# A wider gate product with token-major gates, and three orders moved, in an fp32 hybrid encoder layer

## The chip, the cores and the metric

The kernel runs on one core of a Trainium2 chip. The metric is the device time of one execution in microseconds. A core has a matrix engine (TensorE, PE in the profile; its weight loads are PEld), a vector engine (VectorE, DVE), a scalar engine (ScalarE, ACT), GpSimd (POOL) and SyncE (SP), which here issues nearly all DMAs. Each engine runs its own instructions in order and waits on the others by semaphores. Matrix products land in PSUM, everything else lies in SBUF; what does not fit goes through scratch tensors in DRAM.

## The reference

One encoder layer over 2048 tokens of width 1024, in float32. The input projection's columns go to two groups: group A (width 512) is a gated linear attention that runs in both directions, group B (width 512) a multi-head latent attention with four heads. Each group's output is multiplied by a SiLU gate, both are concatenated, and one output projection and a residual LayerNorm follow:

```python
h = x @ w_in
o_a = gla_branch(g_q, g_k, g_v, g_gate, ...)          # scans both ways, rms_norm, * silu(g_gate)
q  = rms_norm(c_q) @ w_uq;  kv = rms_norm(c_kv) @ w_ukv
p  = softmax(q_nope @ k_nope.T + rope(q_r) @ rope(k_r).T)
o_b = (p @ v) * silu(m_gate)
x  = layer_norm(ALPHA * x + concat(o_a, o_b) @ w_out)
```

The change touches m_gate, the gate of group B: its product with x, its SiLU, and its way to the output stage.

## The kernel before, in words

Every product is done in three matmuls, since each operand is split into a rounded high part and the rest: high·high, low·high and high·low (the helper `mm3`, L419 to L421; `hi` makes a high part on ACT, L365, `lo` the rest on DVE or POOL, L371). Tokens are cut into 16 chunks of 128.

The span has four parts. The first sweep (0 to about 348 us) goes over the chunks backwards and makes group A's inputs and states. The second sweep, `sweep_c` (about 348 to 580 us), takes two chunks at a time in eight steps. The attention (580 to about 1108 us) goes over blocks of 128 queries and pairs of key tiles. The output stage (about 1070 to 1263 us) takes the chunks one by one.

A step of the second sweep works on: `pz`, the gate product, in eight pieces; `ipm`, the product for c_q, c_kv and k_r; `Ob`, the output of group A, whose norm and gate make `og` and its transpose `oT`; `tm`, `cqT_h`, `cqT_l`, the transposed c_q; `pqr` and `pq`, the queries (`qah` and `qal` are the halves of pq). PSUM tiles pz, pq and Ob share a pool `gp` with two slots. The gate goes through ACT three times (`c_gm1` to `c_gm3`: Exp, Ln with bias 1, Exp, which is the sigmoid) and DVE once (`c_gm4`: times pz); `c_sgm` stores it to the scratch `gm_s`. In SBUF, gm and qal share one slot with the tag "gm"; og has two slots of its own.

The order of the second sweep is written as numbers: `PLACE_C` gives each operation a place, the step's number plus an offset (a pair holds the offsets of the step's two chunks, j = 0 and 1); `PLACE_C_FIRST` and `PLACE_C_LAST` replace some of them in the first and the last step. `sweep_c` sorts all operations by place and issues them in that order, and every engine keeps it.

In the output stage, `load` brings a chunk's two halves (`of`, group A from `oa_s` and group B from `ob_s`) and gate factors (`gr`, from `gm_s` and `r_s`, the reciprocal softmax sums) back from DRAM; `load_res` brings x (`xr`). `split` makes high and low parts (`oh`, `ol`) and multiplies by the gate on POOL. `product` runs 48 matmuls of 512 columns for each chunk, into `po` (odd chunks, both halves in one two-bank tile) or into `pmb` and `px` (even chunks, one bank each); `residual` adds x (`rr`), `finish` does the LayerNorm (`ln`) and stores. The last two query blocks' ends are threaded in: `sx` and `rc` (the sums and reciprocals of blocks 14 and 15), `rt` (the transposed reciprocals, made by `turn`), stored by `rows` to `r_s`. From chunk 4 on, `fixed` keeps the written order on ACT, POOL and SP; PE and DVE are placed by the scheduler, which follows an estimate of when things are ready. In the lists of rows below, a name ends in its chunk's, step's or block's number.

Of the kernel before, what the change touches and what calls it, by code (L numbers as in the profile page):

```python
# [135 lines left out]
STEP_C = ("gm1", "gm2", "gm3", "gm4", "sgm", "pq", "qah", "qal", "sqa")  # L136
# [3 lines left out]
    "ss", "rgl", "rgd", "og", "oT", "soT")  # L140
# [57 lines left out]
    gm1=0.823,  # L198
    gm2=0.832,
    gm3=0.837,  # L200
    gm4=0.845,
# [72 lines left out]
    gm1=0.643,  # L274
    gm2=0.815,
    gm3=0.82,
    gm4=0.83,
# [31 lines left out]
    ss=(0.166, 0.454),  # L309
# [4 lines left out]
    krf=(0.139, 0.6),  # L314
# [4 lines left out]
    xl=(-0.244, 0.3),  # L319
# [14 lines left out]
    gm1=1.309,  # L334
    gm2=1.608,
    gm3=1.859,
    gm4=1.953,
# [16 lines left out]
class K:  # L354
# [151 lines left out]
    def run(self):  # L506
        tc, nc, ins = self.tc, self.nc, self.ins
        with ExitStack() as top:
# [9 lines left out]
            self.gm_s = [dp.tile([P, H, QB], F32, name=f"gm_s{b}") for b in range(NQB)]  # L518
# [632 lines left out]
    def sweep_c(self):  # L1151


        with ExitStack() as ctx:
# [9 lines left out]
            def put(n, st, fn, *a, j=None):  # L1164
                last = st == len(steps) - 1
                p = PLACE_C[n]
                p = (last and PLACE_C_LAST.get(n)) or (not st and PLACE_C_FIRST.get(n)) or p
                todo.append((st + (p if j is None else p[j]), len(todo), fn, a))
# [88 lines left out]
    def c_pz(self, s, n):  # L1257
        last = s["st"] == NCH // 2 - 1
        if n == 0:
            s["pz"] = self.gp.tile([P, H, 256], F32, tag="gp", name=f"pz{s['st']}")  # L1260
        order = [(h, k) for h in range(H) for k in range(NK)]
        if last:
            order = [(h, k) for p in range(2) for k in range(NK) for h in (p, p + 2)]
        x2 = lambda t, k: t[:, k].rearrange("p a t -> p (a t)")
        part = [(h, k, p) for h, k in order[4 * n:4 * n + 4] for p in range(3)]
        if n == 0 and s["st"]:

            part.sort(key=lambda e: e[2] == 1)
        stop = {h: (k, p) for h, k, p in part if k == NK - 1}
        for h, k, p in part:  # L1270
            w, x = ((0, self.xch), (0, self.xcl), (1, self.xch))[p]
            self.nc.tensor.matmul(s["pz"][:, h], self.Wz[k][w][:, h * P:(h + 1) * P], x2(x, k),  # L1272
                                  start=(k == 0 and p == 0), stop=stop.get(h) == (k, p))

    def c_gm1(self, s):
        s["gm"] = self.w1.tile([P, H, 256], F32, tag="gm", name=f"gm{s['st']}")
        self.nc.scalar.activation(s["gm"], s["pz"], AF.Exp, scale=-1.0)

    def c_gm2(self, s):
        self.nc.scalar.activation(s["gm"], s["gm"], AF.Ln, bias=1.0)  # L1280

    def c_gm3(self, s):
        self.nc.scalar.activation(s["gm"], s["gm"], AF.Exp, scale=-1.0)

    def c_gm4(self, s):
        self.nc.vector.tensor_tensor(s["gm"], s["pz"], s["gm"], ALU.mult)
# [4 lines left out]
    def c_sgm(self, s):  # L1291
        b, qs = self.of_step(s)
        self.nc.sync.dma_start(self.gm_s[b][:, :, qs], s["gm"])
# [13 lines left out]
    def c_qal(self, s):  # L1307
        s["ql"] = self.w1.tile([P, H, 256], F32R, tag="gm", name=f"qal{s['st']}")
        self.lo(s["ql"], s["pq"], s["qh"])

    def c_sqa(self, s):
        b, qs = self.of_step(s)
        for t, dst in zip((s["qh"], s["ql"]), self.qa_s[b]):
            self.nc.sync.dma_start(dst[:, :, qs], t.bitcast(F32))
# [266 lines left out]
    def attention(self):  # L1581
# [4 lines left out]
        with ExitStack() as ctx:  # L1586
# [284 lines left out]
            with fixed():  # L1871
# [247 lines left out]
```

## Time and profile before

| | |
|---|---|
| median of 3 runs | 1261.82 us (1261.12 to 1262.24) |
| profiled execution | 1264.79 us, of it span 1262.9 |
| granted TensorE clock | 0.997 of full speed |
| PE busy | 1239.1 us, 98% of the span |
| DVE, ACT, POOL busy | 896.3, 729.1, 726.5 us |
| second sweep | about 348 to 580 us |
| output stage's own products | from 1108.87 us |

Read it from PE: where PE is busy without a gap, only its own instructions set the time, and idle time of another engine means nothing. A row of a timeline has the start, the duration, engine, line, operation, output and inputs, shapes, and in brackets the idle time before it with what ended it. A matmul's duration overlaps with its neighbours, so the time that one takes from the engine is the distance between two starts. SPq rows are DMAs as SP issues them.

### The profile page before, as it was taken

How to read it: one execution, taken by the hardware profiler on the slowest of the kernel's cores; microseconds unless marked ns; L12 is line 12 of the kernel's file. 1: busy time of each engine (PE TensorE's matmuls, PEld its weight loads, DVE VectorE, ACT ScalarE, POOL GpSimd, SP SyncE). 2: the span in 40 equal slices, each digit the busy share in tenths (PEclk: the TensorE clock that was granted, in tenths of full speed). 3: DMA queues.
4: the chain of work that ended last, by engine and by line, in shares of the span. 5: the costliest groups of instructions: out<-in, count | busy, mean ns of one | idle time of the engine just before them, and what ended most of it. 6: DMA issues, size and time to landing. Idle time of an engine off the chain costs nothing.

```text
span 1262.9 us, 19554 instructions
## 1 busy us (share of the span) xinstructions
PE 1239.1 (98%) x6848; PEld 1089.6 (86%) x6848; DVE 896.3 (71%) x1666; ACT 729.1 (58%) x1149; POOL 726.5 (58%) x443
## 2 busy tenths in 40 slices
PE   7999999999999999999999999999999999999997
PEld 7999999999899999988788888888888888887886
DVE  6635454554565666665899999999999998378767
ACT  6643434444564444544888888888888888411210
POOL 0132323232355556530798888889999999935551
PEclk9999999999999999999999999999999999999999
DMA  8225555555757788868412222202234110487773
GB/s 294 68 84 130 134 143 139 144 139 144 266 180 212 212 247 244 245 184 210 79 28 49 43 50 43 53 15 59 59 93 93 41 42 26 125 206 212 198 210 100
DMA packets 277393, 165.59 MB, mean 131 GB/s; under 512 B 178630, under 2 KB 234830, under 8 KB 277296
## 3 DMA queue, kind: packets, MB, share of 16 engines
q1 hardware_dynamic: 276176, 162.23, 48.3%
q0 software_dynamic: 672, 2.10, 0.4%
q8 instruction: 54, 0.88, 0.3%
q14 instruction: 43, 0.35, 0.1%
q10 hardware_dynamic: 448, 0.03, 0.0%
HBM read 105.54 MB, written 58.75 MB: 130 GB/s over the span
## 4 chain that ended last, share of the span: by engine, by line
PE 84%; DVE 4%; DMA 4%; POOL 2%; issue 2%; ACT 2%; SPq 1%; DVEq 0%; POOLq 0%; ACTq 0%
PE pz L1272 7%; PE ipm L1341 5%; PE pS L1605 5%; PE pS L1607 4%; PE pS L1606 4%; PE pS L1608 4%; PE pS L1609 4%; PE o L421 4%; PE o L419 4%; PE o L420 4%; PE ipa L419 4%; PE ipa L421 4%; PE ipa L420 4%; PE ipg L421 2%; PE ipg L419 2%
## 5 line engine op out<-in xcount | busy, mean ns | idle before, releaser
L371 POOL TENSOR_TENSOR pl<-s,ph 128x1024 fp32r<-128x1024 f32 x128 | 306.8, 2416 | 47.2 <-ACT ph L365 37.0
L1614 ACT ACTIVATE s<-pS 128x1024 f32<-128x1024 f32 x128 | 131.5, 1028 | 52.9 <-PE pS L1609 49.0
L1627 DVE TENSOR_TENSOR rm<-pS,rm 128x512 f32<-128x512 f32 x210 | 144.6, 689 | 18.3 <-ACT s L1614 12.7
L1651 DVE TENSOR_TENSOR s<-s,mb 128x1024 f32<-128x1024 f32 x128 | 151.2, 1213 | 9.0 <-PE mb L1645 8.9
L365 ACT ACTIVATE ph<-s 128x1024 fp32r<-128x1024 f32 x128 | 134.8, 1056 | 15.7 <-PE o L421 15.1
L1655 ACT ACTIVATE s<-s 128x1024 f32<-128x1024 f32 x128 | 131.6, 1051 | 10.3 <-DVE s L1651 9.6
L419 PE MATMUL ipa<-wah,xah 128*128 128x384 f32 (+1 forms) x384 | 129.2, 336 | 6.1 <-ACT wah L365 6.1
L420 PE MATMUL ipa<-wal,xah 128*128 128x384 f32 (+1 forms) x384 | 125.0, 325 | 0.0
L421 PE MATMUL ipa<-wah,xal 128*128 128x384 f32 (+1 forms) x384 | 124.7, 325 | 0.0
L1091 POOL TENSOR_TENSOR Sb<-Sb,Us 64x512 f32<-64x512 f32 x15 | 19.9, 1327 | 171.5 <-DVE Us L1083 162.3
L1605 PE MATMUL pS<-qh,kvT 128*128 128x512 f32 x256 | 102.6, 401 | 0.8 <-DVE rm L1627 0.4
L419 PE MATMUL o<-ph,vh 128*128 128x512 f32 x256 | 100.9, 394 | 0.0
L1607 PE MATMUL pS<-qh,kvT 128*128 128x512 f32 x256 | 100.0, 391 | 0.0
L1606 PE MATMUL pS<-ql,kvT 128*128 128x512 f32 x256 | 100.0, 390 | 0.0
L421 PE MATMUL o<-ph,vl 128*128 128x512 f32 x256 | 99.8, 390 | 0.0
L1608 PE MATMUL pS<-rh,kvT 128*128 128x512 f32 x256 | 99.8, 390 | 0.0
L1609 PE MATMUL pS<-rl,kvT 128*128 128x512 f32 x256 | 99.8, 390 | 0.0
L420 PE MATMUL o<-pl,vh 128*128 128x512 f32 x256 | 99.7, 389 | 0.0
L1678 DVE TENSOR_TENSOR ap<-ap,s 128x512 f32<-128x512 f32 x120 | 82.9, 691 | 2.7 <-ACT s L1655 0.7
L419 PEld LDWEIGHTS ipa<-wah,xah 128*128 128x128 f32 x384 | 73.3, 191 | 9.3 <-ACT wah L365 6.4
L371 POOL TENSOR_TENSOR ol<-of,oh 128x512 fp32r<-128x512 f32 x32 | 42.5, 1328 | 59.8 <-ACT oh L365 47.4
L1272 PE MATMUL pz<-xch,wzh 128*128 128x256 f32 x256 | 73.4, 290 | 1.4 <-DVE og L1529 1.3
(308 smaller groups left out, 3404.9 us busy)
## 6 DMA issues: line engine op xcount, KB each, us to landing
xcf<-xT_dram SPq DMA_DIRECT2D x16, 512.0 KB, 5.5
xr<-x_dram SPq DMA_DIRECT2D x16, 512.0 KB, 6.0
out_dram<-rr SPq DMA_DIRECT2D x32, 256.0 KB, 3.5
xaf<-xT_dram SPq DMA_DIRECT2D x14, 512.0 KB, 4.2
oib<-oi_s SPq DMA_DIRECT2D x16, 256.0 KB, 4.9
qdb<-qd_s SPq DMA_DIRECT2D x16, 256.0 KB, 3.5
SU<-su_s SPq DMA_DIRECT2D x16, 256.0 KB, 5.0
ub<-u_s SPq DMA_DIRECT2D x16, 256.0 KB, 4.1
```

The source lines that it names most:

```text
L371: return e.tensor_tensor(dst, src, hi.bitcast(F32), ALU.subtract).ins
L419: mm(out, ah, bh, start=start, stop=False)
L420: mm(out, ah, bl, start=False, stop=False)
L421: mm(out, al, bh, start=False, stop=stop)
L1272: self.nc.tensor.matmul(s["pz"][:, h], self.Wz[k][w][:, h * P:(h + 1) * P], x2(x, k), start=(k == 0 and p == 0), stop=stop.get(h) == (k, p))
L1605: mm(ps[:, e], kh, qh, start=True, stop=False)
L1606: mm(ps[:, e], kh, ql, start=False, stop=False)
L1607: mm(ps[:, e], kl, qh, start=False, stop=False)
L1608: mm(ps[:, e], kr, rh, start=False, stop=False)
L1609: mm(ps[:, e], kr, rl, start=False, stop=True)
L1627: V.tensor_tensor(d["rm"], src[:, e], d["rm"], ALU.max)
L1651: V.tensor_tensor(s, s, d["mb"][:, None, :].to_broadcast([P, 2, QB]), ALU.subtract)
```

## The change

The gate product is turned round. Before, a 128x128 piece of the weights is stationary and the x of both chunks moves, 256 columns, so pz has the gate's features on the partitions. Now a chunk's x is stationary and 512 columns of weights move: pz is token-major, [128 tokens, chunk, 512 features], and its eight pieces are four for chunk j = 0 and then four for j = 1. A step has 48 matmuls for it in place of 96.

The three ACT operations and the DVE multiplication are done once per chunk on 128x512, in place of once per step on 128x1024; those of chunk 0 have places before the rest of pz is done. The multiplication writes back into pz, and a new DVE operation, `c_gmx`, transposes it in blocks of 32x32 into gm. The scratch gm_s has one tensor per step; the output stage reads the gate as it reads oa_s, with four DMAs per chunk in rows of 32 elements, where it had one DMA in rows of 128.

qal is made and stored in two halves, in the two slots of og. New places for the step before the last (`PLACE_C_PRE`) and the last step move cqT_l, qrf, ss, krf and xl. In the output stage, chunk 6's split is written ahead of chunk 3's finish, and `turn` and `rows` of block 14 ahead of chunk 6's finish.

```diff
+PLACE_C_PRE = dict(cqTl=(0.758, 1.185), tq=(1.186, 1.56), qrf=(0.853, 1.4305))
...
-    gm1=0.823,
-    gm2=0.832,
-    gm3=0.837,
-    gm4=0.845,
+    gm1=(0.45, 0.823),
+    gm2=(0.46, 0.826),
+    gm3=(0.47, 0.829),
+    gm4=(0.5, 0.832),
+    gmx=(0.76, 0.835),
...
-    xl=(-0.244, 0.3),
+    xl=(-0.244, 0.2),
...
-            self.gm_s = [dp.tile([P, H, QB], F32, name=f"gm_s{b}") for b in range(NQB)]
+            self.gm_s = [dp.tile([2, H, P, P], F32, name=f"gm_s{s}") for s in range(NCH // 2)]
...
-            s["pz"] = self.gp.tile([P, H, 256], F32, tag="gp", name=f"pz{s['st']}")
...
-            self.nc.tensor.matmul(s["pz"][:, h], self.Wz[k][w][:, h * P:(h + 1) * P], x2(x, k),
-                                  start=(k == 0 and p == 0), stop=stop.get(h) == (k, p))
...
+            s["pz"] = self.gp.tile([P, 2, 512], F32, tag="gp", name=f"pz{s['st']}")
+        j, half = divmod(n, 4)
+        for k in (2 * half, 2 * half + 1):
+            xh, xl = self.xch[:, k, j], self.xcl[:, k, j]
+            self.mm3(s["pz"][:, j], xh, xl, self.Wz[k][0], self.Wz[k][1], start=(k == 0), stop=(k == NK - 1))
...
+    def c_gm4(self, d):
+        gm, pz = self.gm(d)
+        self.nc.vector.tensor_tensor(pz, pz, gm, ALU.mult)
+
+    def c_gmx(self, d):
+
+        self.nc.vector.transpose(*self.gm(d))
...
-        s["ql"] = self.w1.tile([P, H, 256], F32R, tag="gm", name=f"qal{s['st']}")
-        self.lo(s["ql"], s["pq"], s["qh"])
+        s["ql"] = []
+        for n in range(2):
+            hs = slice(2 * n, 2 * n + 2)
+            s["ql"].append(self.w1.tile([P, 2, 256], F32R, tag="og", name=f"qal{s['st']}_{n}", bufs=2))
+            self.lo(s["ql"][n], s["pq"][:, hs], s["qh"][:, hs])
...
                     op.residual(rest[c], 0)
                     op.residual(rest[c], 1)
+                    if c == 3:
+                        split(6)
                     op.finish(rest[c])
             for c in range(4, NCH):
                 with fixed():
-                    split(c + 2)
+                    if c > 4:
+                        split(c + 2)
...
                     op.product(rest[c])
+                    if c == 6:
+                        turn(nb - 2)
+                        rows(nb - 2)
                     op.finish(rest[c])
...
-                    if c == 6:
-                        turn(nb - 2)
-                        rows(nb - 2)
...
-        for r, src in kern.blocks_of(kern.oa_s[c].rearrange("h p (m t) -> h p m t", t=32)):
-            nc.sync.dma_start(of[r, 0].rearrange("p h (b t) -> p (h b) t", t=32), src)
-        nc.sync.dma_start(gr[:, 0], kern.gm_s[b][:, :, cs])
+        for dst, scr in ((of, kern.oa_s[c]), (gr, kern.gm_s[c // 2][c % 2])):
+            for r, src in kern.blocks_of(scr.rearrange("h p (m t) -> h p m t", t=32)):
+                nc.sync.dma_start(dst[r, 0].rearrange("p h (b t) -> p (h b) t", t=32), src)
```

How instructions stand in a row, at three places. First DVE in the last steps of the second sweep, before:

```order
L1535 STREAM_TRANSPOSE oT13_6646<-og13_6571 128x512
L1452 STREAM_TRANSPOSE qrx12_6656<-qrf12_6542 128x256
L1546 TENSOR_TENSOR krf14_6658<-ipm14_6560,cos_257 128x64
L1550 TENSOR_TENSOR rope1_14_6659<-ipm14_6560,sin_258 128x32 x2
L1518 TENSOR_REDUCE Ob14_6595<-og14_6663 128x4
L1519 TENSOR_SCALAR ss14_6668<-Ob14_6595 128x4
L371 TENSOR_TENSOR qrT6_6678<-qrx12_6656,qrT6_6678 128x256
L371 TENSOR_TENSOR cqT_l6_6485<-tm13_6665,cqT_h6_6484 128x2x128
```

and DVE at the same place now:

```order
L1547 STREAM_TRANSPOSE oT13_6374<-og13_6299 128x512
L375 TENSOR_TENSOR cqT_l6_6211<-tm13_6386,cqT_h6_6210 128x2x128
L1464 STREAM_TRANSPOSE qrx12_6392<-qrf12_6270 128x256
L1558 TENSOR_TENSOR krf14_6399<-ipm14_6288,cos_261 128x64
L1562 TENSOR_TENSOR rope1_14_6400<-ipm14_6288,sin_262 128x32 x2
```

cqT_l6, which PE's pqr and pq need, moved ahead of the work for chunks 12 and 14. Then DVE in the output stage, at the residual of chunk 2, before:

```order
L2044 SCALAR_TENSOR_TENSOR rr1_11814<-rr1_11814,mv1_11930,lng_11712 128x512 x2
L2032 SCALAR_TENSOR_TENSOR rr2_11969<-xr2_11878,pmb2_11698 128x512
L439 TENSOR_SCALAR ln0_t_11918<-ln0_y_11920,u0_11912 128x1
L439 TENSOR_SCALAR ln1_t_11937<-ln1_y_11939,u1_11931 128x1
L440 TENSOR_SCALAR ln0_t_11918<-ln0_t_11918 128x1
```

and DVE at the same place now:

```order
L2059 SCALAR_TENSOR_TENSOR rr1_11518<-rr1_11518,mv1_11643,lng_11416 128x512 x2
L1747 TENSOR_REDUCE rc15_11939<-sx15_11934 128x4
L1748 RECIPROCAL rc15_11939<-rc15_11939 128x4
L2047 SCALAR_TENSOR_TENSOR rr2_11685<-xr2_11585,pmb2_11402 128x512
L443 TENSOR_SCALAR ln0_t_11631<-ln0_y_11633,u0_11625 128x1
```

rc15 moved ahead of rr2; on PE its input sx15 still follows the last matmul of po3, and pmb4 follows it. Last, SP in the output stage, where the halves and gates of chunk 11 are loaded (gr5 is the buffer of odd chunks), before:

```order
L1754 DMA r_s3_208<-rt14_12317 4x128
L1956 DMA of11_12330<-oa_s11_152 32x16x32 x4
L1957 DMA gr5_11883<-gm_s2_138 128x4x128
L1958 DMA gr5_11883<-r_s2_207 128x4x128
L1959 DMA of11_12330<-ob_s2_211 128x4x128
L1978 DMA xr8_12338<-x_dram 128x1024
```

and SP at the same place now:

```order
L2063 DMA out_dram<-rr6_11991 128x512 x2
L1972 DMA of11_12055<-oa_s11_156 32x16x32 x4
L1972 DMA gr5_11590<-gm_s5_141 32x16x32 x4
L1973 DMA gr5_11590<-r_s2_211 128x4x128
L1974 DMA of11_12055<-ob_s2_215 128x4x128
L1993 DMA xr8_12066<-x_dram 128x1024
```

Four DMAs stand where one stood, ahead of xr8, and the store of rt14's rows moved ahead of chunk 6's stores.

More of the change, by code (lines that the diff above doesn't have):

```diff
@@ L139 @@
     "tq", "qrTh", "qrTl", "Sf1", "Sf2", "M", "Ob", "oib", "sqO",
[L140 removed]
+    "ss", "rgl", "rgd", "og", "oT", "soT", "gm1", "gm2", "gm3", "gm4", "gmx")
 FETCH_C = ("lx", "xh", "xl")
@@ L273 @@
     pz=(-0.249, -0.195, -0.111, -0.018, 0.405, 0.452, 0.485, 0.622),
[L274 to L277, printed above, removed]
+    gm1=(0.53, 0.643),
+    gm2=(0.55, 0.815),
+    gm3=(0.56, 0.82),
+    gm4=(0.61, 0.83),
+    gmx=(0.81, 0.835),
     sgm=1.056,
@@ L333 @@
     pz=(0.572, 0.578, 0.707, 0.845, 0.918, 1.023, 1.1, 1.22),
[L334 to L337, printed above, removed]
+    gm1=(0.9, 1.309),
+    gm2=(0.91, 1.608),
+    gm3=(1.2, 1.859),
+    gm4=(1.26, 1.953),
+    gmx=(1.265, 1.954),
     sgm=2.042,
```

52 lines of the change are left out of this document (24 added, 28 removed).

## The prediction

> **What bounds the kernel now.** I read the page first (busy times and the chain that ended last), then TensorE's own waits, then two windows of the second sweep, then the timelines at the places the change touches.
>
> ```profile
> PE 1239.1 (98%) x6848; PEld 1089.6 (86%) x6848; DVE 896.3 (71%) x1666; ACT 729.1 (58%) x1149; POOL 726.5 (58%) x443
> PE 84%; DVE 4%; DMA 4%; POOL 2%; issue 2%; ACT 2%; SPq 1%; DVEq 0%; POOLq 0%; ACTq 0%
> ...
> PE pz L1272 <- DVE og L1529: 1.3, 2, 0.9
> PE pqr L421 <- DVE cqT_l L371: 1.3, 1, 1.3
> PE ipm L1341 <- POOL xcl L371: 1.0, 1, 1.0
> PE rt L1747 <- ACT rt L1753: 0.8, 1, 0.8
> ...
> 411.00:549.00 138.00, 137.89 (x987) 134.50 (x988) 85.09 (x303) 67.56 (x174) 72.91 (x78) 0.99 0.78 230
> 549.70:564.30 14.60, 11.81 (x76) 10.45 (x74) 13.30 (x54) 6.26 (x21) 4.62 (x7) 1.00 0.70 206
> ```
>
> TensorE is the bound: busy 98% of the span and 84% of the chain. So the change can win in two ways only: fewer or shorter matmuls, and the few waits of which the list here shows some (microseconds in total, times, longest). The two windows (length; then PE, weight loads, DVE, ACT, POOL busy; granted clock; DMA share; GB/s) show where which applies. From 411 to 549, five steps of the sweep, PE is busy 137.89 of 138.00: only matmul time counts and the other engines have room (DVE 85.09). From 549.7 to 564.3, in the last steps, PE has 2.8 us of idle time and DVE is busy 13.30 of 14.60: DVE leads there.
>
> The sum is made against the profiled execution, 1264.79 us (span 1262.9 and 1.9 around it). It is 2.97 above the median of the runs, 1261.82, and I carry that difference over. 0.2%, about what a measurement of this kernel can tell from no change, is 2.5 us.
>
> **Term 1, the gate product.** 768 matmuls with 256 moving columns become 384 with 512, on the same data.
>
> ```profile
> 449.81 2.88 PE pz L1272 x24
> ...
> 222.05 0.39 PE L419 MATMUL ipg<-wgh,xah 128*128 128x512 f32 x1
> ...
> 224.59 0.40 PE L421 MATMUL ipg<-wgh,xal 128*128 128x512 f32 x1
> ...
> 1108.87 0.39 PE L419 MATMUL po<-woh,oh 128*128 128x512 f32 x1
> ...
> 1119.52 0.39 PE L421 MATMUL po<-woh,ol 128*128 128x512 f32 x1
> ```
>
> The chain gives 2.88/24 = 0.120 us for one of today's matmuls. A 512-column matmul of the same three-product form goes from start to start in (224.59 − 222.05)/11 = 0.231 us in the first sweep (twelve matmuls, eleven gaps) and in (1119.52 − 1108.87)/47 = 0.2266 in the output stage. I take 0.231, from the nearer surroundings (a sweep with other forms between). 768 × 0.120 = 92.2 against 384 × 0.231 = 88.7: **−3.5**. Ends: −5.1 at 0.2266, and 0 at 0.240, if a wide one takes just two narrow ones.
>
> The Trainium skill ("TensorE: Matmul & The Clock Gate", Back-to-back issue gap) gives the warm gap as columns / 2.4 GHz + 2.5 ns, so 109.2 and 215.8 ns as estimates; both of this trace's spacings, 120 and 231, lie above, and by the rule the gain would be 768 × 0.1092 − 384 × 0.2158 = 1.0 only. That speaks against the size of this term.
>
> **Term 2, the stall in the third step.** Its chain starts with a buffer.
>
> ```profile
> 400.31 1.03 ACT L1277 ACTIVATE gm<-pz 128x1024 f32<-128x1024 f32 x1 [2.46 <-DMA qr_s<-qrT]
> ...
> 403.55 1.22 DVE L1286 TENSOR_TENSOR gm<-pz,gm 128x1024 f32<-128x1024 f32 x1 [8.78 <-ACT gm L1283]
> ...
> 409.80 0.44 PE L1413 MATMUL tm<-ident,cq 128*128 128x128 f32 x2 [0.83 <-ACT cq L1364]
> ...
> 411.11 0.39 PE L1272 MATMUL pz<-xch,wzh 128*128 128x256 f32 x1 [0.88 <-DVE og L1529]
> ```
>
> ACT's gm waits for a DMA, since qal of the step before lies in the same single slot until its store has landed; DVE stands 8.78 us for gm, does its norm work late, and PE loses 0.83 and 0.88. With qal in the og slots gm1 no longer has that wait, and its first half comes earlier still: **−1.7** (ends 0, if another operation of that step is as late, and −2.4 with the slow matmul behind each wait, since they last 0.44 and 0.39 where the stream goes on in steps of 0.12). What is late next is og, which now follows qal's stores in its two slots:
>
> ```profile
> 478.56 1.22 DVE L371 TENSOR_TENSOR qal<-pq,qah 128x1024 fp32r<-128x1024 f32 x1 [0.43 <-ACT qah L365]
> ...
> 490.66 0.60 ACT L1513 ACTIVATE og<-Ob 128x512 f32<-128x512 f32 x1 [0.48 <-DVE Ob L1509]
> ...
> ql_s<-qal SPq DMA_DIRECT2D x8, 512.0 KB, 4.2
> ```
>
> In a steady step qal ends at 479.78 and og is next written at 490.66, 10.9 us later, while such a store lands in 4.2, so I cost that wait at nothing; if the cover is gone, every step pays what is over.
>
> **Term 3, the new work in the steady steps.**
>
> ```profile
> L1535 DVE STREAM_TRANSPOSE oT<-og 128x512 f32<-128x512 f32 x16 | 11.4, 711 | 0.5
> L1509 DVE TENSOR_TENSOR Ob<-Ob,oib 128x512 f32<-128x512 f32 x16 | 11.1, 693 | 3.3 <-PE Ob L1506 3.3
> L1286 DVE TENSOR_TENSOR gm<-pz,gm 128x1024 f32<-128x1024 f32 x8 | 9.8, 1225 | 45.6 <-ACT gm L1283 45.6
> ```
>
> Per step DVE gains two gmx, a 128x512 transpose like oT (2 × 0.71), two gm4 of about 0.69 in place of one of 1.225, and qal in two halves (about +0.15): +1.7 us. ACT gains the fixed part of three more operations, under 0.7 us. DVE is idle 45.6/8 = 5.7 us a step just ahead of gm4 alone, and half of the gate's work is now done earlier. SP issues one DMA more per step. PE waited for none of them in 138 us: **0**. If a fifth of the 1.7 came through, seven steps would cost 2.4.
>
> **Term 4, the last steps.** The change puts cqT_l6 right behind oT13 (ahead of four DVE operations), Ob15 ahead of qrf13, and xcl15 earlier on POOL.
>
> ```profile
> 563.07 1.12 DVE L1529 SCALAR_TENSOR_TENSOR og<-Ob,rg_r,ub 128x128 f32<-128x128 f32 x4
> ...
> 564.25 0.39 PE L1272 MATMUL pz<-xch,wzh 128*128 128x256 f32 x1 [0.44 <-DVE og L1529]
> ```
>
> The two waits of PE there (1.3 for cqT_l, 1.0 for xcl) go. But PE then needs the slots of the gp pool that og14 and og15 free, the latter at 564.19; DVE has the same work up to there, 13.30 us in 14.60. PE waits for og instead, and the end of the stretch moves only with DVE, by a third of the wait of 0.44 that stands there now: **−0.15** (ends 0 and −2.7, all three waits).
>
> **Term 5, the output stage.** Three moves.
>
> ```profile
> 1119.75 0.60 PE L1724 MATMUL sx<-ident,acc 128*128 128x128 f32 x4
> 1120.10 0.48 PE L419 MATMUL pmb<-woh,oh 128*128 128x512 f32 x1
> ...
> 1119.03 0.69 DVE L2032 SCALAR_TENSOR_TENSOR rr<-xr,pmb 128x512 f32<-128x512 f32 x1 [2.28 <-DMA xr<-x_dram]
> 1127.53 0.63 DVE L1735 TENSOR_REDUCE rc<-sx 128x4 f32<-128x512 f32 x1
> ...
> 1145.29 0.50 PE L419 MATMUL pmb<-woh,oh 128*128 128x512 f32 x1 [0.29 <-ACT oh L365]
> 1147.03 0.50 PE L421 MATMUL pmb<-woh,ol 128*128 128x512 f32 x1 [1.00 <-POOL ol L371]
> ```
>
> rc15's reduction, at 1127.53 today, moves ahead of rr2<-xr2,pmb2 on DVE. It needs sx15 from PE, which starts at 1119.75; today rr2 is done at 1119.72, and pmb4 needs the bank it frees. Now rr2 follows sx (to its end 0.60), the reduction (0.63), then the reciprocal behind it, which I leave out, and takes its own 0.69: 1119.75 + 0.60 + 0.63 + 0.69 = 1121.67 against a start of pmb4 at 1120.10. PE loses **+1.6** (ends 0, if rr2 is not what pmb4 needs, and 2.3, with the 0.69 of another operation between). The split of chunk 6 goes ahead of ln3, so ol6 is there in time: the waits of 1.00 (POOL ol) and 0.29 (ACT oh) go: **−1.3**. rt14 and rt15 are taken early; the listed wait of 0.8: **−0.8**. Together −0.5.
>
> **Term 6, the reload.** gr's half from gm_s comes as four DMAs of 128-byte rows instead of one of 512-byte rows.
>
> ```profile
> 1176.11 1.92 SPq L1956 DMA_DIRECT2D of<-oa_s  x4
> 1178.08 0.54 SPq L1957 DMA_DIRECT2D gr<-gm_s  x1
> ...
> of<-oa_s SPq DMA_DIRECT2D x64, 64.0 KB, 3.9
> gr<-gm_s SPq DMA_DIRECT2D x16, 256.0 KB, 3.4
> ...
> 1165.21 0.69 DVE L2032 SCALAR_TENSOR_TENSOR rr<-xr,pmb 128x512 f32<-128x512 f32 x1 [5.49 <-DMA xr<-x_dram]
> 1186.37 0.69 DVE L2032 SCALAR_TENSOR_TENSOR rr<-xr,pmb 128x512 f32<-128x512 f32 x1 [4.91 <-DMA xr<-x_dram]
> 1228.60 0.69 DVE L2032 SCALAR_TENSOR_TENSOR rr<-xr,pmb 128x512 f32<-128x512 f32 x1 [3.54 <-issue]
> ...
> 1232.86 0.39 PE L419 MATMUL pmb<-woh,oh 128*128 128x512 f32 x1
> ```
>
> Here a loop runs beside PE: rr of an even chunk, its norm, the next split, the reload on SP, xr's load behind it, rr two chunks on. One trip takes 1186.37 − 1165.21 = 21.16 us, a little less than PE's two chunks; the pmb at 1232.86 needs the bank that the rr at 1228.60 frees (1229.29), a margin of 3.57. Four issues of 0.48 in place of one of 0.54 lengthen each trip by d = 1.4 as long as xr is issued behind them on SP; landing adds up to 0.5 more (3.9 against 3.4), and d is 0 if xr's issue does not set rr. I take 1.4, the row of the same pattern on the same queue. Over four trips that is 5.6; PE also comes 0.5 sooner by term 5. So PE waits 5.6 + 0.5 − 3.57: **+2.5** (ends 0 and 4.5).
>
> The Trainium skill ("DMA: Bandwidth & Descriptors", Specifications) wants at least 512 bytes per transfer for line rate; the new rows have 128, which speaks against this part of the change and for the second rival below.
>
> **The sum.** −3.5 − 1.7 + 0 − 0.15 − 0.5 + 2.5 = −3.35: 1264.79 − 3.35 = 1261.4 profiled, and 1258.5 on the scale of the runs.
>
> **Rivals.** *Wide matmuls win nothing.* If one takes 0.238 to 0.240, term 1 is −0.8 to 0 and the sum −0.65 to +0.15: about 1261.5, within 0.2%. For it: the narrow ones run in an unbroken stream at 0.120 already, weight loads hidden. Against it: both 512-column rows lie under 0.240. The Trainium skill's issue-gap rule ("TensorE: Matmul & The Clock Gate", Back-to-back issue gap) ends in this case too, with its gain of 1.0. About the same comes if d is 1.9 (term 6 at 4.5, sum −1.35).
>
> *Slower, by the reload loop.* The place is the even chunks from 6 on, the mechanism that 128-byte rows fill the DMA engines ahead of xr, so that d holds the transfers as well as the issues. The loss is 4d − 3.1 and the other terms are −5.85, so it is as before at d = 2.2 and slower by over 0.2% from d = 2.9; at 3.1 it gives 9.3 − 5.85 = +3.5, or 1265.3. For it: of<-oa_s lands 0.5 later than gr did with a quarter of the bytes, and xr is what rr waits for, 4 to 5.5 us each time. Against it: the issues alone give 1.4, and the last rr shown has no DMA as its releaser.
>
> *All stalls go and nothing follows.* With pmb4 not waiting (term 5 at −2.1), all three waits of the last steps gone (−2.7), the restarts of term 2 won and d under 0.35: −3.5 − 2.4 − 2.7 − 2.1 = −10.7, or 1251.1. For it: each of these waits has a short cause. Against it: DVE's 13.30 of 14.60, and rc15 stands ahead of rr2 in the order.
>
> **How the numbers follow.** Forecast 0.50; nothing won 0.24; slower by the loop 0.18; everything won 0.08. The likeliest gives 1258.5; its own range, with term 1 from −5.1 to −2.5 and d from 0.7 to 1.4, is 1254.4 to 1259.5. The range for 8 in 10 reaches down to the edge of the best case, 1251.5, and up to the near half of the loop's, 1264.8. Faster: 0.50 + 0.08 = 0.58; same 0.24; slower 0.18.
>
> **What would show it.** Term 1: pz matmuls 0.231 apart. Term 2: no wait of gm for a DMA, and none of PE at tm and pz in the third step. Term 3: PE busy all through 411 to 545. Term 4: waits of PE for og in the last steps, 1 to 2 us each, in place of those for cqT_l and xcl. Term 5: PE waiting for DVE's rr at pmb4 and nowhere for ol6 or rt. Term 6: rr8 to rr10 about 22.6 apart and pmb of 12 or 14 waiting for rr. It would be wrong if the wide matmuls come at 0.24, if PE waits in the steady steps for og or gm, or if the trips come out over 24 us.

## The result and the profile after

The changed kernel takes 1269.76 us (median of six runs, 1267.77 to 1272.6) against 1261.6 for the kernel before (six runs, 1260.62 to 1262.24): a ratio of 1.0066, with a 95% interval of 1.0053 to 1.0079. It is slower by 8.2 us, where I had forecast 1258.5 and a gain. Its profiled execution took 1268.82 us with a span of 1267.0 and a mean granted clock of 0.993.

First the page of the changed kernel (busy times and the chain that ended last), then what PE waited for in it (total, times, longest):

```profile
PE 1239.8 (98%) x6464; PEld 1072.6 (85%) x6464; DVE 906.1 (72%) x1698; ACT 733.4 (58%) x1173; POOL 726.1 (57%) x443
PE 89%; DMA 3%; DVE 3%; SPq 3%; ACT 1%; issue 1%; DVEq 0%; ACTq 0%
```

```profile
PE pmb L423 <- DVE rr L2047: 3.7, 2, 3.1
PE pq L423 <- DVE og L1541: 3.1, 2, 2.7
PE pz L423 <- DVE rg_t L447: 2.9, 1, 2.9
...
PE rt L1759 <- DVE rc L1747: 0.8, 1, 0.8
PE pz L423 <- ACT gm L1277: 0.7, 1, 0.7
```

384 matmuls fewer, but PE is as busy as before (1239.8 against 1239.1 us), and SPq, SP's issuing of DMAs, now holds 3% of the chain where it held 1%. The old waits for xcl, cqT_l, ol, oh and cq are gone; a wait at rt of 0.8 is still there, now for DVE's rc in place of ACT's rt. Three new ones of about 3 us each stand in their place. Behind each of them PE also runs slowly for a while, as the windows of the changed kernel show (length; PE, weight loads, DVE, ACT, POOL busy; granted clock; DMA share; GB/s):

```profile
360.00:380.00 20.00, 17.13 (x81) 14.76 (x80) 9.89 (x32) 9.13 (x22) 9.22 (x11) 0.91 0.33 96
411.00:545.50 134.50, 134.42 (x744) 119.71 (x743) 92.92 (x322) 70.80 (x189) 71.86 (x77) 1.00 0.82 238
549.50:562.50 13.00, 10.30 (x62) 9.77 (x60) 11.28 (x47) 4.76 (x15) 3.48 (x5) 0.87 0.67 213
1160.00:1180.00 20.00, 16.94 (x63) 13.40 (x62) 9.54 (x17) 2.42 (x6) 7.30 (x6) 0.83 0.76 195
```

The granted clock is 0.91, 0.87 and 0.83 in the windows with the three waits, and 1.00 in between.

To see where the time lies I take distances between starts of the same matmuls, against a second profile of the kernel before (below; its span is 1258.4). From the first Ob to the first pS of the attention: 220.6 against 217.4 us, so the second sweep lost 3.2. From sx15 to the first matmul of po15: 129.4 against 122.5, so the output stage lost 6.9. The attention between them is equal within 0.1 (539.2 and 539.1). Within the second sweep, the first step lost 4.5 (22.7 against 18.2 from Ob0 to Ob2), the third won 2.0 (27.5 against 29.5), a steady step won 0.18 (27.48 against 27.66), and the last steps lost 1.4. Up to the first Ob the changed kernel is 1.6 us sooner (358.6 against 360.2); 1.3 of that is there already at a wait of the first sweep (335.28 against 336.58), which the change does not touch.

The output stage's loss is at two places. The first is the start of chunk 4. Here is PE's timeline of the changed kernel there (start, duration, what, and idle time before it with its releaser), then DVE's:

```profile
1119.78 0.27 PE L1759 MATMUL rt<-ident,rc 128*4 128x128 f32 x1 [0.78 <-DVE rc L1747]
1120.68 0.47 PE L423 MATMUL pmb<-woh,oh 128*128 128x512 f32 x1 [0.63 <-DVE rr L2047]
```

```profile
1119.03 0.69 DVE L1747 TENSOR_REDUCE rc<-sx 128x4 f32<-128x512 f32 x1 [3.65 <-PE sx L1736]
...
1119.85 0.68 DVE L2047 SCALAR_TENSOR_TENSOR rr<-xr,pmb 128x512 f32<-128x512 f32 x1
```

DVE does rc15 ahead of rr2, and PE waits for both, so that pmb4 starts 2.28 us after sx15 (1118.40 to 1120.68). In both profiles of the kernel before it is 0.35: this place costs 1.9 us. The rest of the loss is at the first matmul of chunk 8, again PE's timeline first, then DVE's and SP's:

```profile
1168.29 0.80 PE L423 MATMUL pmb<-woh,oh 128*128 128x512 f32 x1 [3.06 <-DVE rr L2047]
1168.89 0.63 PE L424 MATMUL pmb<-wol,oh 128*128 128x512 f32 x1
1169.31 0.63 PE L425 MATMUL pmb<-woh,ol 128*128 128x512 f32 x1
```

```profile
1167.55 0.69 DVE L2047 SCALAR_TENSOR_TENSOR rr<-xr,pmb 128x512 f32<-128x512 f32 x1 [9.99 <-DMA out_dram<-rr]
1190.91 0.69 DVE L2047 SCALAR_TENSOR_TENSOR rr<-xr,pmb 128x512 f32<-128x512 f32 x1 [4.86 <-DMA xr<-x_dram]
```

```profile
1154.27 2.77 SPq L1972 DMA_DIRECT2D of<-oa_s  x4
1157.08 2.82 SPq L1972 DMA_DIRECT2D gr<-gm_s  x4
...
1161.05 0.62 SPq L1993 DMA_DIRECT2D xr<-x_dram  x1
```

SP issues from 1154.27 to the load of xr6 at 1161.05 without a gap. In the kernel before that load was issued at 1158.56, although PE was 1.48 us later there (chunk 7 starts at 1154.88, here at 1153.40):

```profile
1158.56 0.62 SPq L1978 DMA_DIRECT2D xr<-x_dram  x1
```

By the page a load of xr lands 6.3 us after its issue (median), xr6 so at about 1167.35, and rr6 follows at 1167.55 (before: 1165.21). The bracket of rr6 names a store in its place, but SP issued that one behind the load, from 1161.76 on. PE stands 3.06 us, and the matmuls after that are 0.42 us apart (1168.89 to 1169.31) where the usual distance is 0.227. The slow stretch lasts until 1174.4 and costs another 2.6 us. The next trip of the loop, to rr8, takes 23.36 us against 21.16 and 21.78 in the two profiles of the kernel before.

The loss in the first step has the following rows, PE first, then ACT and DVE:

```profile
364.87 0.39 PE L425 MATMUL pz<-wzh,xcl 128*128 128x512 f32 x1
368.13 0.50 PE L423 MATMUL pz<-wzh,xch 128*128 128x512 f32 x1 [2.87 <-DVE rg_t L447]
```

```profile
365.29 0.60 ACT L1277 ACTIVATE gm<-pz 128x512 f32<-128x512 f32 x1 [3.53 <-PE pz L425]
...
366.71 0.63 ACT L1285 ACTIVATE gm<-gm 128x512 f32<-128x512 f32 x1
```

```profile
367.38 0.70 DVE L1289 TENSOR_TENSOR pz<-pz,gm 128x512 f32<-128x512 f32 x1
```

The last piece of the gate product for chunk j = 1 starts at 368.13, 0.05 us after the multiplication of chunk 0's gate ends at 368.08, and chunk 0's first ACT operation starts at 365.29, right when the matmul of 364.87 ends, which belongs to chunk 1. They work on different halves of pz, yet each waits for the other: the order that the change wrote (half of the gate between pieces of the product) became a chain. (The bracket of the matmul names rg_t, which DVE ran from 367.99 to 368.14, right behind that multiplication; the run below in which only the gate's half moves shows which of the two it is.)

### The profile page after: what moved, and what is told of

Same layout as the page of the kernel before. It is cut to its first block, busy times and chain, and to the rows that moved or that the text cites. A ratio compares the mean times of both kernels' runs of the same rounds, so it can differ in the third digit from the quotient of the medians.

```text
span 1267.0 us, 18928 instructions
## 1 busy us (share of the span) xinstructions
PE 1239.8 (98%) x6464; PEld 1072.6 (85%) x6464; DVE 906.1 (72%) x1698; ACT 733.4 (58%) x1173; POOL 726.1 (57%) x443
## 4 chain that ended last, share of the span: by engine, by line
PE 89%; DMA 3%; DVE 3%; SPq 3%; ACT 1%; issue 1%; DVEq 0%; ACTq 0%
PE ipm L1353 5%; PE o L423 5%; PE o L425 5%; PE o L424 5%; PE ipa L423 5%; PE pS L1617 4%; PE pS L1619 4%; PE pS L1618 4%; PE pS L1621 4%; PE pS L1620 4%; PE ipa L425 4%; PE ipa L424 4%; PE pz L423 2%; PE ipg L423 2%; PE ipg L425 2%; PE ipg L424 2%
## 5 line engine op out<-in xcount | busy, mean ns | idle before, releaser
L424 PEld LDWEIGHTS ipa<-wal,xah 128*128 128x128 f32 x384 | 73.2, 191 | 0.9 <-DVE wal L375 0.3
```

Of the source, the lines that this page charges most:

```text
L424: mm(out, ah, bl, start=False, stop=False)
```

## The experiments

Each group of runs had its own runs of the kernel before on the same chip: medians 1260.28, 1260.66, 1260.53 and 1260.31 in order of the groups, and 1261.6 beside the changed kernel. The ratios are against these. The changed kernel was not run again in the later groups, so a difference to it in us is uncertain by about 1.3, the difference between these medians.

| run | median us | ratio to before, 95% interval |
|---|---|---|
| changed kernel | 1269.76 | 1.0066 (1.0053 to 1.0079) |
| one reload DMA, wide rows | 1260.9 | 1.0001 (0.9991 to 1.0010) |
| first half of the gate late in all steps | 1295.6 | 1.0281 (1.0266 to 1.0296) |
| last steps' places undone | 1269.73 | 1.0070 (1.0053 to 1.0087) |
| output order undone | 1270.7 | 1.0080 (1.0057 to 1.0102) |
| four reload DMAs, wide rows | 1264.09 | 1.0032 (1.0020 to 1.0044) |
| one reload DMA, narrow rows | 1262.9 | 1.0014 (1.0004 to 1.0023) |
| first half of the gate late in the first step | 1266.17 | 1.0040 (1.0025 to 1.0054) |
| narrow rows moved to the store, and the line above | 1260.7 | 0.9998 (0.9989 to 1.0008) |
| the same, store and last half gate later | 1257.18 | 0.9974 (0.9964 to 0.9984) |
| reload issued by ACT | 1270.53 | 1.0077 (1.0062 to 1.0092) |
| best run with the output order undone | 1257.39 | 0.9980 (0.9967 to 0.9992) |

**The reload.** My theory after the trace was that the reload's loop made most of the loss; the rival put it in the second sweep.

```diff
-        for dst, scr in ((of, kern.oa_s[c]), (gr, kern.gm_s[c // 2][c % 2])):
-            for r, src in kern.blocks_of(scr.rearrange("h p (m t) -> h p m t", t=32)):
-                nc.sync.dma_start(dst[r, 0].rearrange("p h (b t) -> p (h b) t", t=32), src)
+        for r, src in kern.blocks_of(kern.oa_s[c].rearrange("h p (m t) -> h p m t", t=32)):
+            nc.sync.dma_start(of[r, 0].rearrange("p h (b t) -> p (h b) t", t=32), src)
+        nc.sync.dma_start(gr[:, 0], kern.gm_s[c // 2][c % 2].rearrange("h p f -> p h f"))
```

> The changed kernel with the gate reloaded by one DMA of 512-byte rows per chunk in place of four of 128-byte rows (same bytes; the rows are not put back in their order, so the gate's values stand in the wrong places; the time is that of one DMA). Theory A, the loop of the reload is the main loss: the stall of 3.1 us at the matmuls of chunk 8 and the slowed matmuls behind it (2.6 us) go, and the time falls by 5 us, to about 1264.5. Theory B, the main loss is in the second sweep (the wait for half of the gate in the first step, and og in the last steps): the time falls by under 2 us, since chunk 8 then waits for something else.

This run and the next two leave the gate's values in the wrong places; what they tell is the time alone. Measured: 1260.9, 8.8 us less than the changed kernel (7.5 with each taken against its own runs of the kernel before). The whole output stage has no wait of PE left; DVE's rr and SP in this run:

```profile
1161.11 0.69 DVE L2047 SCALAR_TENSOR_TENSOR rr<-xr,pmb 128x512 f32<-128x512 f32 x1 [6.24 <-DMA xr<-x_dram]
1182.10 0.69 DVE L2047 SCALAR_TENSOR_TENSOR rr<-xr,pmb 128x512 f32<-128x512 f32 x1 [4.17 <-DMA xr<-x_dram]
```

```profile
1152.32 0.69 SPq L1972 DMA_DIRECT2D gr<-gm_s  x1
1154.17 0.61 SPq L1993 DMA_DIRECT2D xr<-x_dram  x1
```

xr6 is issued 6.9 us sooner than in the changed kernel, and a trip takes 20.99. Theory A holds, with more than I put on it. A part of that more is not the loop: with this reload DVE has rr2 far ahead of rc15, as in the kernel before, and pmb4 starts 0.35 after sx15 again.

```profile
1116.70 0.69 DVE L2047 SCALAR_TENSOR_TENSOR rr<-xr,pmb 128x512 f32<-128x512 f32 x1 [1.93 <-DMA xr<-x_dram]
...
1126.78 0.63 DVE L1747 TENSOR_REDUCE rc<-sx 128x4 f32<-128x512 f32 x1
```

What in the reload does the rest, the number of DMAs or their rows, the next two runs were to tell apart (the loop over oa_s is as in the run before):

```diff
+        for m in range(4):
+            r = slice(32 * m, 32 * m + 32)
+            nc.sync.dma_start(gr[r, 0], kern.gm_s[c // 2][c % 2].rearrange("h p f -> p h f")[r])
```

> The changed kernel with the gate reloaded by four DMAs per chunk, but in rows of 512 bytes (each a quarter of the partitions; the rows are not put back in their order). Theory A1, the price is the number of DMAs that SP issues: no better than the changed kernel, 1268 to 1271 (the one-DMA reload gave 1260.9). Theory A2, the price is the four times smaller rows on the DMA engines: 1261 to 1263.

```diff
+        nc.sync.dma_start(gr[:, 0].rearrange("p h (b t) -> p (h b) t", t=32),
+                          kern.gm_s[c // 2][c % 2].rearrange("h p f -> (h p f)").rearrange("(k p t) -> p k t", p=P, t=32))
```

> The changed kernel with the gate reloaded by one DMA per chunk, but in rows of 128 bytes (the rows are not put back in their order). Theory A1, the number of DMAs: 1261 to 1263, like the one-DMA reload in wide rows. Theory A2, the small rows: 1267 to 1271.

Measured: 1264.09 with four wide DMAs and 1262.9 with one narrow one, so neither theory alone. Against the single wide DMA, four issues take 3.2 us more, narrow rows 2.0, and both together 8.8 (2.8, 1.6 and 7.5 with each taken against its own kernel before). DVE and SP with four wide DMAs, then with one narrow:

```profile
1164.18 0.69 DVE L2049 SCALAR_TENSOR_TENSOR rr<-xr,pmb 128x512 f32<-128x512 f32 x1 [9.52 <-DMA out_dram<-rr]
```

```profile
1157.84 0.62 SPq L1995 DMA_DIRECT2D xr<-x_dram  x1
```

```profile
1160.84 0.69 DVE L2048 SCALAR_TENSOR_TENSOR rr<-xr,pmb 128x512 f32<-128x512 f32 x1 [7.20 <-DMA xr<-x_dram]
```

```profile
1154.56 0.61 SPq L1994 DMA_DIRECT2D xr<-x_dram  x1
```

These differences are not prices in the loop, though: in neither trace does PE wait at chunk 8. What both runs lose stands ahead of it, at chunk 4, where DVE again has rc15 before rr2. The traces tell the two places apart:

| run | sx15 to pmb4, us | pmb4 to po15, us | load of xr6 behind chunk 6's first matmul, us |
|---|---|---|---|
| one wide DMA | 0.35 | 120.77 | 12.9 |
| one narrow | 2.60 | 120.62 | 13.5 |
| four wide | 2.28 | 121.23 | 15.1 |
| four narrow (changed kernel) | 2.28 | 127.14 | 18.5 |

So in the loop itself narrow rows alone cost nothing that can be told, four issues alone 0.5 us, and only both together 6.4. Four wide DMAs are just in time at chunk 8 (rr6 done at 1164.87, the matmul at 1165.26), and four narrow ones miss it. Why both together delay xr6 by more than the sum of the two was not tried. The trips from rr6 to rr8 (22.39 with four wide, 21.79 with one narrow) can't tell the prices: against 20.99 they look longer by 1.4 and 0.8, but the second profile of the kernel before has 21.78 with its one wide DMA.

The order of rc15 and rr2 follows the reload: rc15 is first in every trace in which SP reloads the gate with four DMAs or in narrow rows, and rr2 in every other one. DVE is placed by the scheduler here, after its estimate of when things are ready; that the estimate for the reload decides it is likely, but not shown.

One more way was to take the issues off SP, with the rows as changed.

```diff
-        for dst, scr in ((of, kern.oa_s[c]), (gr, kern.gm_s[c // 2][c % 2])):
+        for eng, dst, scr in ((nc.sync, of, kern.oa_s[c]), (nc.scalar, gr, kern.gm_s[c // 2][c % 2])):
...
-                nc.sync.dma_start(dst[r, 0].rearrange("p h (b t) -> p (h b) t", t=32), src)
+                eng.dma_start(dst[r, 0].rearrange("p h (b t) -> p (h b) t", t=32), src)
```

> The changed kernel with the four DMAs per chunk that reload the gate issued by ACT in place of SP; rows and order in the program as changed, and the result in its right order. If SP's issuing is the greater part of the loss: 1262 to 1264, like one DMA in small rows (1262.9), or less, since SP then issues less than before the change. If ACT now stands for the buffers that these DMAs write: waits of PE for oh or ln, and 1270 or more.

Measured: 1270.53, no gain. PE stands 5.2 us at chunk 8. On ACT the DMAs follow a split's second half, which itself waits for POOL, so they are issued late:

```profile
1163.03 0.63 ACT L369 ACTIVATE oh<-of 128x512 fp32r<-128x512 f32 x1 [6.31 <-POOL of L1980]
1163.04 1.97 ACTq L1972 DMA_DIRECT2D gr<-gm_s  x4
```

So this run does not isolate SP's issuing; it shows that the place in an engine's order can cost as much as the issues did.

**The half gate.**

```diff
-    gm1=(0.45, 0.823),
-    gm2=(0.46, 0.826),
-    gm3=(0.47, 0.829),
-    gm4=(0.5, 0.832),
+    gm1=(0.56, 0.823),
+    gm2=(0.562, 0.826),
+    gm3=(0.564, 0.829),
+    gm4=(0.568, 0.832),
...
-    gm1=(0.53, 0.643),
-    gm2=(0.55, 0.815),
-    gm3=(0.56, 0.82),
-    gm4=(0.61, 0.83),
+    gm1=(0.625, 0.643),
+    gm2=(0.63, 0.815),
+    gm3=(0.635, 0.82),
+    gm4=(0.64, 0.83),
...
-    gm1=(0.9, 1.309),
-    gm2=(0.91, 1.608),
-    gm3=(1.2, 1.859),
+    gm1=(1.221, 1.309),
+    gm2=(1.222, 1.608),
+    gm3=(1.223, 1.859),
```

> The changed kernel with the three ACT operations and the multiplication of the gate's first chunk placed behind the last piece of the gate product in every step. Theory B, the second chunk's product waits for the first chunk's gate because both lie in one PSUM tile: the stall of 2.9 us in the first step, the slow matmuls behind it (1.5 us), the 0.18 us in each of six steps and the 0.7 us in the last step go, and the time falls by 5 us, to about 1264.5. Theory A, that stall is only a symptom of late DVE work in the first step: PE waits for og or for a slot at the next product instead, and the time falls by under 1.5 us.

Measured: 1295.6, 26 us worse. The wait of the first step is gone, but every steady step has new ones:

```profile
PE pqr L425 <- DVE cqT_l L375: 8.5, 5, 1.7
PE tm L1425 <- ACT cq L1376: 8.1, 5, 1.6
PE pz L423 <- DVE og L1541: 5.8, 6, 1.1
```

The mistake was mine: placed behind the pieces in the order but still far ahead of the other half, the first half's gate now waits for the whole product (ACT stands 4.10 us for it in one of the steps, DVE 9.02 for ACT), and ACT and DVE, in order, hold cq, cqT_l and og behind it. It confirms the coupling of the halves without giving its price. The price comes from moving the first step's half gate alone, to where the second half stands:

```diff
-    gm1=(0.53, 0.643),
-    gm2=(0.55, 0.815),
-    gm3=(0.56, 0.82),
-    gm4=(0.61, 0.83),
-    gmx=(0.81, 0.835),
+    gm1=(0.64, 0.643),
+    gm2=(0.81, 0.815),
+    gm3=(0.818, 0.82),
+    gm4=(0.825, 0.83),
+    gmx=(0.832, 0.835),
```

> The changed kernel with the first chunk's gate in the first step placed where the second chunk's stands (as in the kernel before), all other steps as changed. If the second chunk's product waits for the first chunk's gate because both lie in one tile, the wait of 2.9 us in the first step and the 1.5 us of slow matmuls behind it go, and nothing else moves: 4 us faster than the changed kernel, 1265 to 1266.5. If DVE's late work is behind it: within 1 us of the changed kernel, PE waiting for og in the first step.

Measured: 1266.17, 3.6 us less than the changed kernel, as expected (2.6 with each taken against its own kernel before); the wait of 2.9 us is not in its list. In its trace the second sweep is 3.9 us shorter (216.7 against 220.6).

**The orders.** The last two steps' places, and the output stage's order, each undone alone:

```diff
-PLACE_C_PRE = dict(cqTl=(0.758, 1.185), tq=(1.186, 1.56), qrf=(0.853, 1.4305))
+PLACE_C_PRE = {}
...
-    ss=(0.188, 0.454),
+    ss=(0.166, 0.454),
...
-    krf=(0.187, 0.6),
+    krf=(0.139, 0.6),
...
-    xl=(-0.244, 0.2),
+    xl=(-0.244, 0.3),
```

> The changed kernel with the last two steps' places as they were before (cqT_l, tq, qrf, ss, krf, xl). If the new places of the last steps cost what the trace shows there (one wait of 2.7 us for og and 1.4 us of slow matmuls behind it, against three short waits of 2.8 us in all and no slow stretch): the time falls by 1 to 2 us, to about 1268. If they win as they stand and the wait for og is there in either order: the time rises by 1 to 2.5 us.

```diff
-                    if c == 3:
-                        split(6)
...
-                    if c > 4:
-                        split(c + 2)
+                    split(c + 2)
...
-                    if c == 6:
-                        turn(nb - 2)
-                        rows(nb - 2)
                     op.finish(rest[c])
...
+                    if c == 6:
+                        turn(nb - 2)
+                        rows(nb - 2)
```

> The changed kernel with the output stage's order as it was before (chunk 6's split, and the rows of blocks 14 and 15). If the reload's loop sets the stall at chunk 8 whatever the order: within 1 us of the changed kernel, with waits for ol6 and rt back and the stall at chunk 8 shorter by as much. If the order is what makes rr6 late: the time falls by 3 to 5 us. If the order wins what I forecast: the time rises by 0.5 to 2 us.

Measured: 1269.73 and 1270.7, neither to be told from the changed kernel. With the last steps' places as before, their old waits are back, in the timeline of PE:

```profile
554.35 0.39 PE L425 MATMUL pqr<-wqr_h,cqT_l 128*128 128x256 f32 x1 [1.53 <-DVE cqT_l L375]
556.93 0.67 PE L1353 MATMUL ipm<-wmh,xcl 128*128 128x448 f32 x2 [1.03 <-POOL xcl L375]
563.58 0.50 PE L423 MATMUL pz<-wzh,xch 128*128 128x512 f32 x1 [0.63 <-DVE og L1541]
```

Three waits of 3.2 us in all against one of 2.7: the new places change which operation PE waits for. At chunk 8 PE then waits 4.4 us in place of 3.1, so this run can't price the last steps alone. With the output order undone, PE waits 3.1 us for oh and ol and 1.2 at rt, and the wait at chunk 8 is down to 0.3: the late reload is paid at another place. DVE's order at chunk 4 is not changed by it:

```profile
1119.78 0.69 DVE L1747 TENSOR_REDUCE rc<-sx 128x4 f32<-128x512 f32 x1 [3.62 <-PE sx L1736]
...
1120.64 0.69 DVE L2044 SCALAR_TENSOR_TENSOR rr<-xr,pmb 128x512 f32<-128x512 f32 x1
```

The order of the output stage was tried again where the reload no longer hides it, on the best run (next):

> The run with the later store (1257.2, all matmuls of the output stage without a wait) with the output stage's order as it was before: chunk 6's split behind chunk 3's finish, rows of block 14 behind chunk 6's finish. If the moved orders win what the waits of the kernel before show (0.3 + 1.0 for ol6 and oh6, 0.8 for rt in one profile, 0.5 + 0.4 in the other): 1258 to 1259.3, with these waits back. If with a quicker reload or other shifts they are hidden anyway: 1256.5 to 1257.7, no difference that can be told.

Measured: 1257.39 against 1257.18, no difference. With the old order there is no wait at all in the output stage here, so the new order has nothing left to win.

**A version that beats both.** The narrow rows are moved to the store, in the second sweep, eight DMAs a step; the output stage reloads with one wide DMA in the right order.

```diff
-        self.nc.sync.dma_start(self.gm_s[s["st"]].rearrange("j h p f -> p (j h) f"),
-                               s["gm"].rearrange("p j (h f) -> p (j h) f", h=H))
+        for j in range(2):
+            dst = self.gm_s[s["st"]][j].rearrange("h (m i) (a t) -> a i (h m) t", i=32, t=32)
+            for a in range(4):
+                self.nc.sync.dma_start(dst[a], s["gm"][32 * a:32 * a + 32, j].rearrange("i (k t) -> i k t", t=32))
```

> The small rows moved to the other side: the second sweep stores the gate in eight DMAs of 128-byte rows per step, so that the output stage reloads it with one DMA of 512-byte rows per chunk, in its right order; and the first step's gate as in the run before. If SP and the DMA engines have room for it in the second sweep (DMA share 0.8 there): the gains of the one-DMA reload and of the first step add up, 1260.9 - 4 = 1257, faster than the kernel before by 3 us. If they have not: waits for loads or for the gate's slot come up in the steady steps, and the time is 1262 or more.

Measured: 1260.7, no better than the kernel before. The steady steps bear the eight stores without a wait, but in the last steps they stand on SP ahead of the load of ub14, and PE stands 5.2 us for og. SP and DVE in this run:

```profile
546.51 5.26 SPq L1302 DMA_DIRECT2D gm_s<-gm  x8
551.82 0.50 SPq L1481 DMA_DIRECT2D ub<-u_s  x1
```

```profile
555.04 1.13 DVE L1543 SCALAR_TENSOR_TENSOR og<-Ob,rg_r,ub 128x128 f32<-128x128 f32 x4 [3.37 <-DMA ub<-u_s]
```

So two places more were moved:

```diff
-PLACE_C_PRE = dict(cqTl=(0.758, 1.185), tq=(1.186, 1.56), qrf=(0.853, 1.4305))
+PLACE_C_PRE = dict(sgm=1.66, cqTl=(0.758, 1.185), tq=(1.186, 1.56), qrf=(0.853, 1.4305))
...
-    gm1=(0.9, 1.309),
-    gm2=(0.91, 1.608),
-    gm3=(1.2, 1.859),
+    gm1=(1.221, 1.309),
+    gm2=(1.222, 1.608),
+    gm3=(1.223, 1.859),
```

> The run with the scattered store, and in it two places moved: the gate's store of the step before the last goes behind the two loads of ub that stood after it on SP, and the last step's first half of the gate goes behind the last piece of the gate product. If the wait of 5.2 us for og in the last steps (with 1.6 us of slow matmuls behind it) comes from ub14, which SP issued after the eight stores, it falls to 2 to 2.5 us, and the 0.7 us for gm in the last step goes: 1260.7 - 4.5 = 1256, faster than the kernel before by 4 us. If og is late by DVE's own work: 1259 to 1261.

Measured: 1257.18, 0.9974 of the kernel before (0.9964 to 0.9984), 3.3 us faster than it and 12.6 faster than the changed kernel. What is left of PE's waits in the second sweep is mainly this; pmb has no line any more, and the half gate one of 0.2 us:

```profile
PE pq L423 <- DVE og L1543: 2.2, 2, 1.8
PE pz L423 <- DVE og L1543: 1.8, 2, 0.9
```

**The kernel before, profiled again.**

> The kernel before, profiled again, to see which of its waits belong to every execution. If the stall in the third step (1.7 us) with slow matmuls behind it (1.5 us) belongs to the kernel, it is there again, and the profiled time is near 1264.8. If it came from a late DMA of that one execution, it is gone, and the profiled time lies near the median of the runs, 1260.5.

Measured: 1260.25 us, and the third step's waits are there again (0.47 for cq, 0.87 for og), but without slow matmuls behind them; the waits in the output stage are shorter (0.5 for ol, 0.4 for rt, none for oh).

```profile
PE pmb L421 <- POOL ol L371: 0.5, 1, 0.5
PE tm L1413 <- ACT cq L1364: 0.5, 1, 0.5
...
PE rt L1747 <- ACT rt L1753: 0.4, 1, 0.4
```

So the waits belong to the kernel, with their lengths varying, and the profile that I worked from was an execution 4.5 us longer than this one.

## Why the prediction was wrong

Two steps failed: the margin and the wait in term 6, and term 3, which put the half gate at nothing.

**Term 6, the reload.** Its mechanism was right: the loop of rr, split, reload and xr, lengthened by d per trip. The trips came out as forecast, 23.36, 22.80 and 22.27, on average 22.8 against 22.6, so d is 1.7 (22.81 against 21.13; 1.3 against the 21.50 of the second profile), and the rival "slower, by the reload loop", which needed 2.2, had the sign right but not the condition. What failed is where the margin stands. I let the loop start on time at rr6 and set four trips against the 3.57 at its end. But the reloads ahead of xr6 pay already: its load is issued 18.5 us behind chunk 6's first matmul, where it was 16.6 and 15.3 in the two profiles of the kernel before. The margin that counts is the one at chunk 8, 0.54 in the first profile (rr6 done at 1165.90, the first matmul of chunk 8 at 1166.44). PE waited 3.06 there. I also charged a wait at its length, while PE ran at half speed for 5.5 us behind it and lost 2.6 more. And I put the rows' share at nothing: alone they cost nothing in the loop, but with four wide DMAs PE has no wait at chunk 8, with four narrow ones it has. Forecast +2.5; against the single wide DMA the traces show 6.4 in the loop, and the 1.9 at chunk 4, which I had under term 5, came with the reload too.

The sentence that I quoted against it, that the Trainium skill ("DMA: Bandwidth & Descriptors", Specifications) wants 512 bytes per transfer, is borne out here in direction only with four DMAs: their narrow transfers land later (a median of 2.5 us against 2.1), and the loop loses 6.4 us where the wide ones lose 0.5. One DMA lands in 4.2 us with narrow rows and in 4.0 with wide ones, and the loop shows no loss.

**Term 3 missed a wait.** I costed the half gate's early place at nothing because ACT and DVE have room. I didn't ask what it adds on PE: in this kernel an operation on one half of a PSUM tile, written between matmuls into the other half, made these wait. It cost 3.6 us in the first step by the run, and by the trace about 0.18 in each steady step and 0.69 in the last.

**Term 1 was right in mechanism and half eaten.** The wide matmuls come 0.227 to 0.235 apart: in steady steps 96 × 0.120 = 11.52 us became 48 × 0.229 to 0.235, or 11.0 to 11.3, and the step is 0.18 us shorter where I expected 0.43. The half gate's wait takes 0.17 of that. The 0.216 of the Trainium skill's issue-gap rule ("TensorE: Matmul & The Clock Gate", Back-to-back issue gap) was not reached.

**Term 2 was right:** no wait of gm for a DMA, none of PE at tm and pz in the third step, 2.0 us less in it than in the second profile of the kernel before (forecast 1.7), and 3.9 less than in the first, which had 1.5 us of slow matmuls there; og's wait for qal's store doesn't show.

**Term 4 was right in kind:** PE waits for og in place of cqT_l and xcl. Undone, the time is the same within its interval (forecast −0.15); by the trace the last steps lost 1.4 us, as much as the slow matmuls behind the wait for og. That og14 was also held by its load of ub, behind the gate's store on SP, I had not seen.

**Term 5:** pmb4 starts 2.28 us after sx15 where it was 0.35: +1.9, forecast +1.6, by DVE's order as I had read it. But this is not a price of the three moves: with the moves undone it is 2.33, and with the single wide DMA, moves in place, 0.35. The waits for ol6 and oh6 are gone as forecast. The −0.8 for rt did not come: its old wait for ACT is gone, but it now waits 0.78 for rc15, inside the 1.9. Together the moves win nothing that can be measured (−0.5 forecast), since the old waits vary and vanish with other shifts.

The sum as it came out, from medians of different groups and so to about 1 us: the reload +8.8 and the first step's half gate +3.6 leave −4.2 for all the rest of the 8.2; with each run taken against its own kernel before (7.5 and 2.6) they leave −2.0. Terms 1 to 5 as forecast made −5.85. The best run, with both removed and the store's price paid, has −3.3.

## What to carry to other kernels

Before a transfer is cut into more DMAs, look at the queue that issues it: where it already issues without a gap ahead of a load that something waits for, further issues delay that load (here by 2.2 us with four wide DMAs, by 5.6 with four narrow ones), and what counts is the margin at the first place that needs it. The same DMAs cost nothing that could be measured at another place (here: at the store, in a sweep with room, and behind the loads that are due first). When a run changes more than one thing in the trace, take the stages apart before a difference of medians is called a price: here an edit of the reload also turned two DVE operations round. Before a consumer of half a tile is placed between the writes of the other half, make sure that the halves are tracked apart; if they are not, early is late. And charge a wait of the matrix engine with more than its length when it is several microseconds long.

## What the hardware showed that I had not expected

After a wait of PE its matmuls may come at half speed for 3 to 5.5 us, though not always. In the changed kernel, all three long waits had it: 2.87 us with 1.5 us lost behind it, 2.70 with 1.4, 3.06 with 2.6. From 1168.9 to 1174.2, behind the last of them, the granted clock is 0.50. Seven profiles have the wait of 2.87 in the first step, and six of them the slow stretch (1.2 to 1.5 us lost); the run with one narrow DMA has none. The wait of 1.8 for og has a slow stretch (1.6 us lost) in the run with the old output order and none in the best run, which has the same wait. The two waits of the third step of the kernel before, 0.83 and 0.88, had 1.5 us of it in the first profile and, at 0.47 and 0.87, none in the second. Why the same wait does it in one execution and not in another was not tried. The Trainium skill ("TensorE: Matmul & The Clock Gate", What's actually happening) describes a clock that is halved after an idle window of about 3.4 us, where the window runs freely. The halved clock agrees with the 0.50 and with matmuls 0.42 in place of 0.227 us apart. The length does not: each of these waits is shorter than 3.4 us, and most of them had a slow stretch behind them. No run here shows the window itself.
